# Feed-forward down product: all eleven pairs of k tiles by seven products, in three rounds

## The chip, the cores and the metric

The kernel runs on one core of one Trainium2 chip. The metric is the device time of one execution in microseconds (us). The core has a matrix engine (PE, with its weight loads shown as PEld), a vector engine (DVE), a scalar engine (ACT), a general engine (POOL) and a queue engine that only starts transfers (SP). Each of them executes its own list of instructions in a fixed order; semaphores hold an instruction back until what it needs is there.

## The reference, cut to what matters

The program is a trunk of two layers on 512 tokens of width 1024: a state-space mixer (SSD), a feed-forward block (FFN), latent attention (MLA), and a second FFN. After every block the residual stream `h` is normalised.

```python
def conv_ffn(h, up, conv_w, conv_b, down):          # hidden width 2816
    u = causal_depthwise_conv(h @ up, conv_w, conv_b)
    g, val = jnp.split(u, 2, axis=-1)
    return (jax.nn.silu(g) * val) @ down

for i in range(DEPTH):                               # DEPTH = 2
    mix = ssd_mixer(...) if i < N_A_LAYERS else mla_attention(...)
    h = layer_norm(DN_ALPHA * h + mix, ln_mix_g[i], ln_mix_b[i])
    ff = conv_ffn(h, ffn_up[i], ffn_conv_w[i], ffn_conv_b[i], ffn_down[i])
    h = layer_norm(DN_ALPHA * h + ff, ln_ffn_g[i], ln_ffn_b[i])
```

The change is in the product with `down`, 512 tokens x 2816 x 1024, in both FFN blocks, and in the normalisation that follows it.

## The kernel before, in words

**Precision.** Every product is made of three matmuls: each operand is kept as a rounded high part and a low remainder (hi, lo), and hi x hi, hi x lo and lo x hi are added in PSUM. `mm_b` (L162) issues these three for one stationary tile of 128 tokens and 512 output columns. Its first matmul needs the high part of the weight, its second the low part.

**The weight stream.** `WStream` (L31) walks one long list of items, the weights in the order in which products use them. SP loads an item into one of six staging buffers. `_split` (L76) makes the high part on ACT (L96, a cast) and the low part on DVE (L97, a subtraction) in one of six pairs of buffers (`nb`), and then `fill` (L59) starts further loads. `ahead(i)` (L102) splits items up to `la` (4) places beyond `i`, but never more than six beyond the last retired item. `retire` (L112) wants the items in order.

**The hidden width.** 2816 is 22 k tiles of 128. For each k tile the kernel makes two products with `up`, the convolution and the gate (`conv3_silu_gate`, L321, called by `finish`).

**Seven products for a pair.** An even and an odd k tile, two halves of the tokens (256 each) and two halves of the output columns (512 each) form a 2 x 2 by 2 x 2 block product. It is done with seven products instead of eight. `pair_operands` (L344) makes the operands a11, a12, a22, s1, s2, s3, s4 on the token side. On the weight side the operands are sums, kept in the tiles `rs` (`sums`), one for each part of a round (a part is one or two pairs that share an item). The kinds of an item say how it arises: "r" is loaded into `rs`; "a" is added to `rs` by an accumulating DMA which POOL issues (L52); "+" is added on DVE (L88); "=" uses the loaded tile itself; "-" is `rs` minus the loaded tile on DVE (L91); no kind is a plain load. An accumulating DMA can start only when every reader of `rs` before it is done.

**The rounds.** `RP0` and `RP1` (L288) give two rounds: five pairs in parts of 2, 2 and 1, then four pairs in parts of 2, 1 and 1. `down_pairs` (L361) runs a round: a11, s1, s2 and s4 in turn, s3, a12, a22, each over all parts, and adds each result to `h` on DVE (L387). Its inner `ahead` wraps the splits in `issue_after(ins)`, so that their DVE instructions come behind the add just issued. The last four k tiles have no pairs: after round two they are multiplied plainly, one token tile after another and the two column halves in turn (L525 to L555), with the items of 1024 columns held for all four token tiles. Each of these adds (`add_mix`, L175, L185) also sums the row for the mean.

**Normalisation.** For token tile i: `ln_mean` (L189, DVE), a square with a row sum on ACT (L194), `ln_a` (two halves on DVE, L210), the variance (L203, on DVE in the second FFN, on POOL in the first) and a power on POOL (L204), then `ln_b` (two halves, L215), which stands behind the first add of the next token tile. In the first FFN `transpose_h` (L266) turns a finished tile by eight PE transposes (L274) into `ht`, with a cast on ACT (L277) and a subtraction on DVE (L278); the last two transposes are done inside MLA. MLA's first product, `down(0)` (L1155), reads tile 0 of `ht`, the third matmul already its low part. In the second FFN the last token tile goes through `ln_last` (L231), which takes its second column half as two matmul groups of 256 columns, adds them at L243 and L251, and ends the kernel.

**Order.** SP's list is in the order of the program text. The lists of the other engines are made by a planner at compile time: whenever an engine is free in its plan, the ready instruction that stands first in the program text goes next. `issue_after` forbids the instructions in its block, on that one engine, to stand ahead of the given instruction.

Of the kernel before, what the change touches and what calls it, by code (L numbers as in the profile page):

```python
# [18 lines left out]
P = 128  # L19
# [11 lines left out]
class WStream:  # L31
# [5 lines left out]
    def __init__(self, k, items, nb, nst, la):  # L37
        self.k, self.items, self.nb, self.nst, self.la = k, items, nb, nst, la
        self.out = 0
        self.split = 0  # L40
        self.done = 0
        self.st = {}
        self.w = {}

# [67 lines left out]
    def retire(self, i):  # L112
        assert i == self.done
        del self.w[i]
        self.done += 1
# [172 lines left out]
RP0 = ((2, 2, 1), (2, 1, 1))  # L288
RP1 = ((2, 2, 1), (2, 1, 1))


def rounds(rp):
    r0 = 2 * sum(rp[0])
    return r0, r0 + 2 * sum(rp[1])


def ffn_items(up, down, rp):
# [3 lines left out]
    it = []  # L301
    R0, R1 = rounds(rp)
    dv = down.rearrange("(k p) n -> p k n", p=P)
    for r, ks in enumerate((range(R0), range(R0, HT))):
        for c in ks:
            it.append((up[c], 1024))
            it.append((up[c + HT], 1024))

        for odd, hf, kinds in ((0, 0, "r"), (0, 1, "a"), (1, 1, "+="), (0, 0, "-"), (1, 0, None), (1, 0, "a")):
            j = ks[0]  # L310
            for p, n in enumerate(rp[r]):
# [49 lines left out]
def down_pairs(k, ws, n, prs, parts, first, between):  # L361

    nc = k.nc
    X, Y, Z = ([k.bank() for _ in range(2)] for _ in range(3))
    ni = len(parts)
    at = [sum(parts[:p]) for p in range(ni + 1)]
    new = {(i, hf) for i in range(NT) for hf in range(2)} if first else set()  # L370

    def product(bs, op, p, i, start, stop):
        wh, wl = ws.get(i, 3)
        ps = prs[at[p]:at[p + 1]]
        for t in range(2):
            for q, pr in enumerate(ps):
                x, c0 = pr[op]
                sl = slice(q * 512, (q + 1) * 512)
                k.mm_b(bs[t], x, slice(c0 + t * P, c0 + (t + 1) * P), wh[:, sl], wl[:, sl],
                       start and p == 0 and q == 0, stop and p == ni - 1 and q == len(ps) - 1)  # L380
        ws.retire(i)

    def add(bs, row, hf, sign):
        for t in range(2):
            i = 2 * row + t
            hs = k.h[:, i, hf * 512:(hf + 1) * 512]
            last = nc.vector.scalar_tensor_tensor(hs, hs, ALPHA if (i, hf) in new else 1.0, bs[t], op0=ALU.mult,  # L387
                                                  op1=ALU.add if sign > 0 else ALU.subtract)
            new.discard((i, hf))
        return last  # L390

    def ahead(n, ins):

        with k.tc.issue_after(ins.ins):
            ws.ahead(n)

    for p in range(ni):
        product(X, "a11", p, n + p, True, True)
    n += ni
    ahead(n, add(X, 0, 0, 1))  # L400
    for p in range(ni):
        product(Y, "s1", p, n + p, True, True)
    n += ni
    ahead(n, add(Y, 1, 1, 1))
    between()
    for p in range(ni):
        product(X, "s2", p, n + 2 * p, False, True)
        product(Y, "s4", p, n + 2 * p + 1, False, True)
    n += 2 * ni
    add(X, 0, 1, -1)  # L410
    ahead(n, add(Y, 0, 1, 1))
    for bs, op, s0, out in ((X, "s3", False, (1, 1, -1)), (Z, "a12", True, (0, 0, 1)), (X, "a22", False, (1, 0, 1))):
        for p in range(ni):
            product(bs, op, p, n + p, s0, True)
        n += ni
        ahead(n, add(bs, *out))
    return n


def ffn(k, ws, base, cwp, gb, rp, la=2, out=None, mid=None):  # L420

    nc, tc = k.nc, k.tc
    R0, R1 = rounds(rp)
    with ExitStack() as c:
        pool = lambda n, b: c.enter_context(tc.tile_pool(name=n, bufs=b))
        pools = {"gt": pool("gt", 18), "fw": pool("fw", 7), "rs": pool("rs", 1), "cw": pool("cw", 1)}
# [8 lines left out]
        ws.sums = [rs[:, 0], rs[:, 1], pools["rs"].tile([P, 512], F32, name="rs2")]  # L435
# [9 lines left out]
        for r in range(2):  # L445
            gts, prs = [], []
# [4 lines left out]
            def finish(ci, bg, bv):  # L451
                if ci >= R1:
                    gts.append(new_gt())
                    conv3_silu_gate(k, pools, bg, bv, cw, ci, gts[-1])
                    return
# [10 lines left out]
            c0 = r * R0  # L466
# [21 lines left out]
            for ci in range(c0, HT if r else R0):  # L488
# [11 lines left out]
            n = down_pairs(k, ws, n, prs, rp[r], not r, norm_params if r else lambda: None)  # L500
        if out is None:
            k.new_ht()

        nk = HT - R1
        nw = nk // 2

        def piece(i, b, hf, c0, c1, retire):
            for jc in range(nw):
                wh, wl = ws.get(n + hf * nw + jc)
                for jj in range(2):  # L510
                    j = jc * 2 + jj
                    o = slice(jj * 512 + c0, jj * 512 + c1)
                    k.mm_b(b, gts[j], slice(i * P, (i + 1) * P), wh[:, o], wl[:, o], j == 0, j == nk - 1)
                if retire:
                    ws.retire(n + hf * nw + jc)

        xn = {}
# [961 lines left out]
```

## Time and profile before

| | |
|---|---|
| median of 3 runs | 1307.37 us (1306.93 to 1308.01) |
| time of the profiled execution | 1306.91 us |
| its span, first to last instruction | 1305.2 us |
| mean granted clock of TensorE | 0.998 |
| instructions: PE, DVE, ACT, POOL | 6570, 1605, 1022, 88 |
| bytes moved by DMA | 147.72 MB, 113 GB/s on average |

The profile is one execution. A row of its timeline has the start in us, the busy time in us, the engine, the line of the kernel, the operation, what it writes and reads, and the count of merged instructions; in brackets stands the idle time before it and what ended that. A row of its view by windows has the stretch, its length, the busy time (and count) of PE, PEld, DVE, ACT and POOL, the granted clock of TensorE, the mean busy share of the DMA engines and GB/s.

### The profile page before, as it was taken

To read this page: it belongs to the slowest core of one execution; us is meant where nothing else is said; L and a number is where in the kernel's file an instruction comes from. 1 tells how busy PE (TensorE), PEld (TensorE's weight loads), DVE (VectorE), ACT (ScalarE), POOL (GpSimd) and SP (SyncE) were. 2 spreads that over 40 slices of the span, in tenths; PEclk is the share of its full clock that TensorE was granted. 3 is DMA by queue.
4 is the path that set the end of the run, shared out by engine and by line. 5 is a ranking of instruction groups with operands and counts; after the bars stand their busy time and mean duration, and the time that the engine had idled before them with its cause. 6 is when DMAs were issued, how large, how long until landed. Compare 5 with 4: busy or idle time off the path is not lost.

```text
span 1305.2 us, 17262 instructions
## 1 busy us (share of the span) xinstructions
PE 1296.5 (99%) x6570; PEld 1100.7 (84%) x6570; DVE 1008.0 (77%) x1605; ACT 630.7 (48%) x1022; POOL 67.5 (5%) x88
## 2 busy tenths in 40 slices
PE   9999999999999999999999999999999999999997
PEld 8888888888888988888888899888898888888886
DVE  7788888787799868866766876898587786667587
ACT  6766545536533544444443434665254444444341
POOL 0000000000001001100000012000100000000000
PEclk9999999999999999999999999999999999999999
DMA  8533323324411433352312721231054226333251
GB/s 298 192 125 114 142 101 102 131 73 144 161 62 68 130 129 81 76 206 95 126 63 33 249 89 61 70 109 49 17 180 137 69 40 208 129 97 105 41 162 64
DMA packets 52082, 147.72 MB, mean 113 GB/s; under 512 B 5568, under 2 KB 8640, under 8 KB 50720
## 3 DMA queue, kind: packets, MB, share of 16 engines
q1 hardware_dynamic: 46784, 136.71, 30.5%
q0 software_dynamic: 5072, 9.77, 4.4%
q8 instruction: 51, 0.84, 0.3%
q14 instruction: 31, 0.25, 0.1%
q10 hardware_dynamic: 144, 0.15, 0.0%
HBM read 144.44 MB, written 2.16 MB: 112 GB/s over the span
## 4 chain that ended last, share of the span: by engine, by line
PE 99%; DVE 0%; issue 0%; ACT 0%; DVEq 0%; ACTq 0%
PE ps L159 58%; PE ps L165 10%; PE ps L167 10%; PE ps L166 10%; PE ps L1276 2%; PE ps L800 1%; PE ps L1317 1%; PE ps L925 1%; PE ps L274 1%; PE ps L816 1%; PE ps L1299 1%; PE ps L789 1%; PE ps L743 1%; PE ps L767 1%; PE ps L620 0%; PE ps L838 0%
## 5 line engine op out<-in xcount | busy, mean ns | idle before, releaser
L159 PE MATMUL ps<-ht,wh 128*128 128x512 f32 (+1 forms) x2256 | 517.1, 379 | 0.0
L159 PEld LDWEIGHTS ps<-ht,wh 128*128 128x128 f32 x2256 | 408.1, 188 | 79.6 <-issue 1.4
L97 DVE TENSOR_TENSOR wl<-wst,wh 128x1024 fp32r<-128x1024 f32 (+3 forms) x222 | 253.4, 1158 | 39.8 <-ACT wh L96 38.7
L96 ACT CAST wh<-wst 128x1024 fp32r<-128x1024 f32 (+3 forms) x222 | 218.7, 995 | 125.3 <-PE ps L167 68.5
L159 PE MATMUL ps<-ht,wl 128*128 128x512 f32 (+1 forms) x1128 | 266.7, 379 | 0.0
L159 PEld LDWEIGHTS ps<-ht,wl 128*128 128x128 f32 x1128 | 205.2, 188 | 39.7
L328 DVE SCALAR_TENSOR_TENSOR acc<-ps,cw,acc 128x511 f32<-128x511 f32 x88 | 65.7, 747 | 80.1 <-ACT acc L327 80.1
L165 PE MATMUL ps<-wh,gt 128*128 128x512 f32 (+1 forms) x320 | 123.7, 387 | 0.0
L167 PE MATMUL ps<-wh,gt 128*128 128x512 f32 (+1 forms) x320 | 123.6, 386 | 0.0
L166 PE MATMUL ps<-wl,gt 128*128 128x512 f32 (+1 forms) x320 | 123.6, 386 | 0.0
L340 ACT CAST gt<-acc 128x512 fp32r<-128x512 f32 (+1 forms) x80 | 44.0, 571 | 101.9 <-DVE acc L333 99.3
L327 ACT ACTIVATE acc<-ps,cw 128x512 f32<-128x512 f32 x88 | 68.3, 776 | 29.5 <-PE ps L159 29.4
L658 DVE SCALAR_TENSOR_TENSOR cv<-ps,cw,cv 128x511 f32<-128x511 f32 (+2 forms) x72 | 53.7, 745 | 21.7 <-ACT cv L656 21.1
L166 PEld LDWEIGHTS ps<-wl,gt 128*128 128x128 f32 x320 | 60.1, 188 | 12.2
L165 PEld LDWEIGHTS ps<-wh,gt 128*128 128x128 f32 x320 | 60.1, 188 | 12.2
L167 PEld LDWEIGHTS ps<-wh,gt 128*128 128x128 f32 x320 | 60.1, 188 | 12.1
L332 ACT ACTIVATE acc<-acc 128x512 f32<-128x512 f32 x44 | 27.8, 632 | 87.6 <-DVE acc L329 87.4
L329 DVE SCALAR_TENSOR_TENSOR acc<-ps,cw,acc 128x510 f32<-128x510 f32 x88 | 65.8, 747 | 2.5
L96 ACT CAST wh<-rs 128x1024 fp32r<-128x1024 f32 (+1 forms) x48 | 39.9, 834 | 46.1 <-DVE rs L88 27.1
L341 DVE TENSOR_TENSOR gt<-acc,gt 128x512 fp32r<-128x512 f32 (+1 forms) x80 | 48.7, 627 | 13.5 <-ACT gt L340 13.5
L387 DVE SCALAR_TENSOR_TENSOR h<-h,ps 128x512 f32<-128x512 f32 x56 | 37.5, 685 | 25.6 <-PE ps L167 25.6
L52 POOL DMA_DIRECT2D rs<-in_down_dram x24 | 25.1, 1045 | 576.1 <-DVE wl L97 576.1
(248 smaller groups left out, 1727.2 us busy)
## 6 DMA issues: line engine op xcount, KB each, us to landing
wst<-in_up_dram SPq DMA_DIRECT2D x88, 512.0 KB, 3.5
wst<-in_xbc_dram SPq DMA_DIRECT2D x32, 512.0 KB, 6.3
wst<-in_down_dram SPq DMA_DIRECT2D x26, 512.0 KB, 5.8
W<-cumd SPq DMA_DIRECT2D x8, 1024.0 KB, 4.7
wst<-in_sow_dram SPq DMA_DIRECT2D x16, 512.0 KB, 3.5
wst<-in_zw_dram SPq DMA_DIRECT2D x14, 512.0 KB, 6.0
rs<-in_down_dram POOLq DMA_DIRECT2D x12, 512.0 KB, 6.9
wst<-in_down_dram SPq DMA_DIRECT2D x18, 256.0 KB, 2.6
```

Source lines behind the costliest of these rows:

```text
L96: nc.scalar.copy(h[:, :f], s[:, :f])
L97: nc.vector.tensor_tensor(l[:, :f], s[:, :f], h[:, :f], op=ALU.subtract)
L159: nc.tensor.matmul(out, w[:, k, :], xts[k][:, x, ts], start=first and p == 0 and k == 0, stop=last and p == 2 and k == nk - 1, skip_group_ ...
L165: nc.tensor.matmul(out, xt[:, 0, tsl], wh, start=start, stop=False, skip_group_check=True)
L166: nc.tensor.matmul(out, xt[:, 0, tsl], wl, start=False, stop=False, skip_group_check=True)
L167: nc.tensor.matmul(out, xt[:, 1, tsl], wh, start=False, stop=stop, skip_group_check=True)
L327: nc.scalar.activation(a, b, AF.Identity, bias=cw[:, ch, 3:4], scale=cw[:, ch, 2:3])
L328: nc.vector.scalar_tensor_tensor(a[:, 1:], b[:, :SEQ - 1], cw[:, ch, 1:2], a[:, 1:], op0=ALU.mult, op1=ALU.add)
L329: nc.vector.scalar_tensor_tensor(a[:, 2:], b[:, :SEQ - 2], cw[:, ch, 0:1], a[:, 2:], op0=ALU.mult, op1=ALU.add)
L340: k.nc.scalar.copy(dst[:, 0, :], src)
L341: k.nc.vector.tensor_tensor(dst[:, 1, :], src, dst[:, 0, :], op=ALU.subtract)
L658: nc.vector.scalar_tensor_tensor(t[:, d:], b[:, :SEQ - d], cw[:, ch, 3 - d:4 - d], t[:, d:], op0=ALU.mult, op1=ALU.add)
```

## The change

All 22 k tiles become eleven pairs, in three rounds of four, three and four pairs, in parts (2, 2), (2, 1) and (2, 2). The plain product of the last four k tiles is gone, and with it the third tile of sums. `down_pairs` becomes a class `Pairs`. In every round a11 and s1 are now interleaved part by part, so the items are no longer retired in order, and `retire` allows that. In the last round the column halves are exchanged and the items of a12 stand ahead of those of s3. That round ends one token tile at a time: a12 for tiles 0 and 1, then s3 and a22 for tile 2, s3 and a22 for tile 3, where a22 starts in banks of its own. The normalisation is placed between these. `ln_last` is kept.

```diff
     def retire(self, i):
-        assert i == self.done
         del self.w[i]
-        self.done += 1
+        self.gone.add(i)
+        while self.done in self.gone:
+            self.gone.remove(self.done)
+            self.done += 1
...
-RP0 = ((2, 2, 1), (2, 1, 1))
-RP1 = ((2, 2, 1), (2, 1, 1))
+RP = ((2, 2), (2, 1), (2, 2))
...
+HEAD = ((0, 0, "r"), (0, 1, "a"), (1, 1, "+="))
+TAIL = ((0, 0, "-"), (1, 0, None), (1, 0, "a"))
...
+        last = r == len(rp) - 1
+        for odd, hf, kinds in HEAD + ((TAIL[1], TAIL[0], TAIL[2]) if last else TAIL):
+            j = at[r]
+            hf = 1 - hf if last else hf
...
-    for hf in range(2):
-        for j in range(R1, HT, 2):
-            it.append((dv[:, j:j + 2, hf * 512:(hf + 1) * 512], 1024))
...
+    def ahead(self, ins):
+
+        with self.k.tc.issue_after(ins.ins):
+            self.ws.ahead(self.n)
+
+    def half(self, between, f, last=False):
+
+        X, Y, ni = self.X, self.Y, self.ni
         for p in range(ni):
-            product(bs, op, p, n + p, s0, True)
-        n += ni
-        ahead(n, add(bs, *out))
-    return n
+            self.product(X, "a11", p, self.n + p, True)
+            if p == ni - 1:
+                a = self.adds(X, 0, f, 1)
+                with self.k.tc.issue_after(a.ins):
+                    self.ws.ahead(self.n + 2 * ni - 1)
+            self.product(Y, "s1", p, self.n + ni + p, True)
+        self.n += 2 * ni
+        self.ahead(self.adds(Y, 1, 1 - f, 1))
+        between()
+        for p in range(ni):
+            self.product(X, "s2", p, self.n + 2 * p, False)
+            self.product(Y, "s4", p, self.n + 2 * p + 1, False)
+        self.n += 2 * ni
+        self.adds(X, 0, 1 - f, -1)
+        self.ahead(self.adds(Y, 0, 1 - f, 1, last))
...
+            if r < len(rp) - 1:
+                pp = Pairs(k, ws, n, prs, rp[r], not r)
+                pp.half(lambda: None, 0)
+                n = pp.rest()
...
+        pp = Pairs(k, ws, n, prs, rp[-1], False)
+        ni = pp.ni
+        pp.half(norm_params, 1, True)
+        for t in range(2):
+            for p in range(ni):
+                pp.tile(pp.Z[t], "a12", p, pp.n + p, t, True)
+                if t:
+                    ws.retire(pp.n + p)
+            a = pp.add(pp.Z[t], t, 1, 1, True)
+            if t:
+                with tc.issue_after(a.ins):
+                    ln_b(0, 0)
+                    ln_b(0, 1)
+            ln_a(t)
+        pp.n += ni
+        pp.ahead(a)
+        for t in range(2):
+            i = 2 + t
+            for p in range(ni):
+                pp.tile(pp.X[t], "s3", p, pp.n + p, t, False)
+                if t:
+                    ws.retire(pp.n + p)
+            pp.add(pp.X[t], i, 0, -1, True)
+            a = pp.add(pp.X[t], i, 1, 1)
+            with tc.issue_after(a.ins):
+                ln_b(i - 1, 0)
+                if out is None or not t:
+                    ln_b(i - 1, 1)
+            if t:
+                with tc.issue_after(a.ins):
+                    ws.ahead(pp.n + 2 * ni, la)
+                if out is None:
+                    k.transpose_h(0)
+            cuts = ((0, 256), (256, 512)) if t and out is not None else ((0, 512),)
+            bs = [k.bank()[:, :c1 - c0] for c0, c1 in cuts]
+            for b, (c0, c1) in zip(bs, cuts):
+                for p in range(ni):
+                    pp.tile(b, "a22", p, pp.n + ni + p, t, True, c0, c1)
+                    if t and c1 == 512:
+                        ws.retire(pp.n + ni + p)
+            if len(bs) > 1:
+                k.ln_last(i, bs, out[i * P:(i + 1) * P, :], lambda: ln_b(i - 1, 1))
+                continue
+            if t:
+                ws.ahead(pp.n + 2 * ni, la)
+            pp.add(bs[0], i, 1, 1, True)
+            if t:
+                k.transpose_h(1)
+            ln_a(i)
```

The method `tile` issues the matmuls of one part for one token tile, `add` adds one bank to `h` (with the row sum if `last`), `adds` does so for both tiles of a product, and `rest` runs s3, a12 and a22 of the first two rounds as before.

More of the change, by code (lines that the diff above doesn't have):

```diff
@@ L358, in pair_operands @@
     split(k, s34, v)
[L361 to L374, printed above, removed]
-        for t in range(2):
[L376 to L383, printed above, removed]
-        for t in range(2):
[L385 to L398, printed above, removed]
-    n += ni
[L400 to L412, printed above, removed]
-        for p in range(ni):
-            product(bs, op, p, n + p, s0, True)
-        n += ni
-        ahead(n, add(bs, *out))
-    return n
@@ new lines, with __init__, tile, product @@
+class Pairs:
+    def __init__(self, k, ws, n, prs, parts, first):
+        self.k, self.ws, self.n, self.prs, self.parts, self.first = k, ws, n, prs, parts, first
+        self.ni = len(parts)
+        self.at = [sum(parts[:p]) for p in range(self.ni + 1)]
+        self.new = {(i, hf) for i in range(NT) for hf in range(2)} if first else set()
+        self.X, self.Y, self.Z = ([k.bank() for _ in range(2)] for _ in range(3))
+    def tile(self, out, op, p, i, t, start, c0=0, c1=512):
+        wh, wl = self.ws.get(i, 3)
+        ps = self.prs[self.at[p]:self.at[p + 1]]
+        for q, pr in enumerate(ps):
+            x, o = pr[op]
+            sl = slice(q * 512 + c0, q * 512 + c1)
+            self.k.mm_b(out, x, slice(o + t * P, o + (t + 1) * P), wh[:, sl], wl[:, sl],
+                        start and p == 0 and q == 0, p == self.ni - 1 and q == len(ps) - 1)
+    def product(self, bs, op, p, i, start):
+        for t in range(2):
+            self.tile(bs[t], op, p, i, t, start)
+        self.ws.retire(i)
+    def add(self, b, i, hf, sign, last=False):
+        k = self.k
+        kw = {}
+        if last:
+            if i not in k.st:
+                k.st[i] = k.small.tile([P, 6], F32, name="lnst", bufs=4)
+            kw["accum_out"] = k.st[i][:, hf:hf + 1]
+        hs = k.h[:, i, hf * 512:(hf + 1) * 512]
+        a = k.nc.vector.scalar_tensor_tensor(hs, hs, ALPHA if (i, hf) in self.new else 1.0, b, op0=ALU.mult,
+                                             op1=ALU.add if sign > 0 else ALU.subtract, **kw)
+        self.new.discard((i, hf))
+        return a
+    def adds(self, bs, row, hf, sign, last=False):
+        for t in range(2):
+            a = self.add(bs[t], 2 * row + t, hf, sign, last)
+        return a
+    def ahead(self, ins):
[3 more added lines that the diff above has]
+        X, Y, ni = self.X, self.Y, self.ni
+        for p in range(ni):
+            self.product(X, "a11", p, self.n + p, True)
[13 more added lines that the diff above has]
+        self.ahead(self.adds(Y, 0, 1 - f, 1, last))
+    def rest(self):
+        for bs, op, s0, out in ((self.X, "s3", False, (1, 1, -1)), (self.Z, "a12", True, (0, 0, 1)), (self.X, "a22", False, (1, 0, 1))):
+            for p in range(self.ni):
+                self.product(bs, op, p, self.n + p, s0)
+            self.n += self.ni
+            self.ahead(self.adds(bs, *out))
+        return self.n
@@ L487, in ffn @@
                 c0 += 2
-            for ci in range(c0, HT if r else R0):
+            for ci in range(c0, at[r + 1]):
                 bg, bv = k.bank(), k.bank()
```

90 lines of the change are left out of this document (27 added, 63 removed).

## The prediction

> **What bounds the kernel now.** I read the page first: the busy shares and the chain of waits.
>
> ```profile
> PE 1296.5 (99%) x6570; PEld 1100.7 (84%) x6570; DVE 1008.0 (77%) x1605; ACT 630.7 (48%) x1022; POOL 67.5 (5%) x88
> ...
> PE 99%; DVE 0%; issue 0%; ACT 0%; DVEq 0%; ACTq 0%
> ```
>
> PE never pauses, so every matmul removed can shorten the run. But DVE is at 77% on average, and the windows view shows where it stands higher: the up stage before round two, round two, and the plain tail with its normalisation, in the first FFN.
>
> ```profile
> 577.40:707.90 130.50, 130.50 (x577) 108.12 (x576) 88.19 (x122) 56.72 (x78) 2.92 (x3) 1.00 0.32 98
> 707.90:746.00 38.10, 38.10 (x169) 31.56 (x169) 30.83 (x40) 17.96 (x23) 2.96 (x3) 1.00 0.59 182
> 746.00:769.50 23.50, 23.50 (x114) 19.61 (x112) 20.46 (x38) 9.16 (x13) 2.65 (x6) 1.00 0.29 94
> ```
>
> After the stretch and its length, the first busy time is PE's and the third is DVE's: 88 of 130, 31 of 38, and 20.5 of 23.5 in the tail. The change takes PE time out of that last stretch, so the question is whether DVE can follow.
>
> The timeline of PE gives the price of a matmul and the fixed points of the second FFN: round two starts at 1237.43, the last token tile's half-width matmuls at 1294.55, the last one at 1297.30.
>
> ```profile
> 1237.43 0.39 PE L165 MATMUL ps<-wh,gt 128*128 128x512 f32 x1
> ...
> 1294.55 0.28 PE L165 MATMUL ps<-wh,gt 128*128 128x256 f32 x1
> ...
> 1297.30 0.28 PE L167 MATMUL ps<-wh,gt 128*128 128x256 f32 x1
> ```
>
> Four pairs are 7 x 4 x 2 x 3 = 168 matmuls, the tail up to 1294.55 has 84: 57.12 / 252 = 0.2267 us each. The 23 steps to the last one give 0.12 for half width.
>
> **The change: what PE saves.** Four plain k tiles cost 4 x 4 x 2 x 3 = 96 matmuls, two pairs 84. Two FFNs save 24 x 0.2267 = 5.44 us. Nothing else is taken from PE.
>
> **What DVE gains, and where.** Call E the end of s4 in the last round. Before, PE had 72 matmuls of pairs and 96 of the tail left after s4, 38.1 us. Now it has 72 in all: 16.3 us. Into these go the normalisation of tiles 0 to 2 and, by the order of the text, weight splits. The DVE timeline of the second FFN shows the rule by which splits are placed.
>
> ```profile
> 1234.19 0.68 DVE L88 TENSOR_TENSOR rs<-rs,wst 128x512 f32<-128x512 f32 x1
> ...
> 1242.47 1.28 DVE L387 SCALAR_TENSOR_TENSOR h<-h,ps 128x512 f32<-128x512 f32 x2
> 1243.67 1.22 DVE L88 TENSOR_TENSOR rs<-rs,wst 128x1024 f32<-128x1024 f32 x1
> 1244.93 1.23 DVE L91 TENSOR_TENSOR wst<-rs,wst 128x1024 f32<-128x1024 f32 x1
> 1246.08 1.23 DVE L97 TENSOR_TENSOR wl<-rs,wh 128x1024 fp32r<-128x1024 f32 x1
> 1247.22 1.22 DVE L97 TENSOR_TENSOR wl<-wst,wh 128x1024 fp32r<-128x1024 f32 x1
> ...
> 1257.35 2.73 DVE L387 SCALAR_TENSOR_TENSOR h<-h,ps 128x512 f32<-128x512 f32 x4 [0.65 <-PE ps L167]
> 1259.99 1.82 DVE L97 TENSOR_TENSOR wl<-wst,wh 128x1024 fp32r<-128x1024 f32 x2
> ```
>
> The sum of part 1 (512 wide, 1234.19) ran nine us ahead of that of part 0 (1243.67), because only the latter is split inside the `issue_after` of the a11 adds (1242.47). Likewise the splits at 1259.99 stand right behind the four adds of s2 and s4. E was 1237.43 + 96 x 0.2267 = 1259.19, so the last of these adds ended at E + 0.89 (1260.08).
>
> I number the items of the new last round 0 to 13: a11 0, 1; s1 2, 3; s2 and s4 4 to 7; a12 8, 9; s3 10, 11; a22 12, 13. While s4 runs, `get` with look-ahead 3 reaches item 10. Items 11 and 12 come from `ahead` behind the s4 adds, 13 from `ahead` behind the second a12 add. So after E + 0.89 DVE has one L91 (item 11) and three L97: 1.15 + 3 x 1.14 = 4.57 us, by the steps 1244.93 to 1246.08 to 1247.22. Then come adds and normalisation:
>
> ```profile
> 1269.59 1.37 DVE L387 SCALAR_TENSOR_TENSOR h<-h,ps 128x512 f32<-128x512 f32 x2 [1.73 <-PE ps L167]
> 1270.87 1.22 DVE L97 TENSOR_TENSOR wl<-wst,wh 128x1024 fp32r<-128x1024 f32 x1
> ...
> 1281.15 0.69 DVE L185 SCALAR_TENSOR_TENSOR h<-h,ps 128x512 f32<-128x512 f32 x1 [2.02 <-PE ps L167]
> ...
> 1281.88 0.21 DVE L189 TENSOR_SCALAR lnst<-lnst 128x1 f32<-128x1 f32 x1
> 1282.13 1.42 DVE L210 SCALAR_TENSOR_TENSOR xn<-h,lnst,lng 128x512 f32<-128x512 f32 x2
> 1283.46 0.15 DVE L203 TENSOR_SCALAR lnst<-lnst 128x1 f32<-128x1 f32 x1
> ...
> 1296.18 0.42 DVE L243 SCALAR_TENSOR_TENSOR h<-h,ps 128x256 f32<-128x256 f32 x1
> ...
> 1297.87 0.41 DVE L251 SCALAR_TENSOR_TENSOR h<-h,ps 128x256 f32<-128x256 f32 x1
> ```
>
> An add with mean, `ln_a` and variance is 1281.15 to 1283.61, 2.46 us. Two adds are 1.28, and 0.08 more with a row sum (the subtracting add with a row sum has no row; its price lies between 0.64 and the 0.73 of L185, I take 0.72). An `ln_b` pair is 1.32 (767.94 to 769.26, below).
>
> **Second FFN, in DVE's order from E:** 0.89; weights 4.57; tile 0 2.46; tile 1 with `ln_b` of tile 0 3.78; two s3 adds and `ln_b` 2.68; tile 2 2.46; two s3 adds and half an `ln_b` 2.02; from L243 to L251 1.69 as before. That is 20.55. Every piece is there by its turn (PE delivers tile 1 at 5.44, s3 of tile 2 at 8.2), so DVE does not pause. PE alone would allow L251 at 60 x 0.2267 + 24 x 0.12 + 0.45 (1297.42 to 1297.87) = E + 16.93. DVE is late by 3.62, and the end moves with L251.
>
> **First FFN.** `down(0)` follows the last transposes on PE, and its third matmul needs the low part of tile 0 of `ht`.
>
> ```profile
> 768.69 1.03 PE L274 MATMUL ps<-ident,h 128*128 128x128 f32 x8
> 769.48 0.42 PE L165 MATMUL ps<-wh,ht 128*128 128x384 f32 x1
> ...
> 769.91 0.34 PE L167 MATMUL ps<-wh,ht 128*128 128x384 f32 x1
> ```
>
> ```profile
> 764.21 1.28 DVE L278 TENSOR_TENSOR ht<-ps,ht 128x512 fp32r<-128x512 f32 x2
> 765.40 0.74 DVE L210 SCALAR_TENSOR_TENSOR xn<-h,lnst,lng 128x512 f32<-128x512 f32 x1
> ...
> 767.94 1.41 DVE L215 SCALAR_TENSOR_TENSOR h<-xn,lnst,lnb 128x512 f32<-128x512 f32 x2
> 769.26 2.95 DVE L97 TENSOR_TENSOR wl<-wst,wh 128x1024 fp32r<-128x1024 f32 x3
> 772.14 0.68 DVE L185 SCALAR_TENSOR_TENSOR h<-h,ps 128x512 f32<-128x512 f32 x1
> 772.74 1.28 DVE L278 TENSOR_TENSOR ht<-ps,ht 128x512 fp32r<-128x512 f32 x2
> ```
>
> Before, the low part of tile 0 was there at 765.4, 4.5 us ahead of its use, and the add and transposes of the last tiles could stand behind three splits (769.26) at no cost. Now tile 0's transposes stand behind `ws.ahead(..., la)`, in the text after s3 of tile 3. In DVE's order: 0.89; weights 4.57; four more L97 for MLA's first items (14 to 17) 4.56; tile 0 2.31 (no L203 on DVE here); tile 1 and `ln_b` 3.63; s3 adds and `ln_b` 2.68; tile 2 2.31; s3 adds and `ln_b` 2.68; the first L278 0.60: E + 24.2. PE alone would reach `down(0)` at 16.32 + 2 x 0.79 = E + 17.9 and its third matmul 0.43 later (769.48 to 769.91). DVE is late by 5.90.
>
> Sum, on the profiled execution: 1306.91 - 5.44 + 3.62 + 5.90 = 1310.99. The median lies 0.46 above that execution: **1311.5 us**.
>
> **The accumulating DMA of a22.** Item 13 reaches `rs` by a DMA that waits for L91 of item 11, at E + 2.04.
>
> ```profile
> 1244.98 1.06 ACT L96 CAST wh<-rs 128x1024 fp32r<-128x1024 f32 x1 [3.15 <-DVE rs L88]
> ...
> 1247.69 1.20 POOL L52 DMA_DIRECT2D rs<-in_down_dram  x1 [23.88 <-DVE wl L97]
> ...
> DMA to landing us min/median/max: 3.9/6.5/9.3
> ```
>
> POOL starts 0.38 after the DVE end (1247.31), landing takes 6.5 (3.9 to 9.3), the cast 1.06, L97 1.2: E + 11.6 (9.0 to 14.4). PE wants the low part after 43 matmuls, E + 9.75, so it waits up to 4.7, likely 1.9, in each FFN. DVE's list has L97 of item 13 done at 11.7 anyway, so this wait lies inside the lateness above; it costs 3.8 in all only if DVE keeps pace. Behind item 13's cast on ACT stand the squares, and behind its L97 on DVE the s3 adds: with a landing of 9.3 DVE stands for up to 14.4 - 11.7 = 2.7 more, and with 3.9 for nothing.
>
> **What I cost at nothing.** The other rounds: a round of (2, 2) keeps 38.1 us of PE and gets some 33 of DVE (the 30.8 above, with the last pair's operands in and less narrow splits out); one of (2, 1) has 28.6 of PE and about 29 of DVE, and the surplus falls into an up stage with 42 us free (577.40). Without that cover the cost is 1 us a round. s1 of part 0 is now wanted 2.7 us after the start, but its items are split a whole up tile (10.9) earlier. s2 reuses the banks of a11, whose adds must be done; 1 us remains in the (2, 1) round. On SP the normalisation's two loads stand behind MLA's item loads, which wait for L97 to free staging; that eats the margin in the first FFN only, and late they would add to DVE's lateness.
>
> **Rivals.** (a) The clock. In the first FFN, with the 1.9 of the a22 wait, PE is through its transposes at about E + 19.8 and stands some 4 us until E + 24.2. What an idle PE does is seen after the last matmul:
>
> ```profile
> 1299.40:1300.40 1.00, 0.00 (x0) 0.00 (x0) 1.00 (x2) 0.00 (x0) 0.84 (x1) 0.90 0.12 45
> 1300.40:1301.40 1.00, 0.00 (x0) 0.00 (x0) 1.00 (x3) 0.00 (x0) 0.00 (x0) 0.50 0.00 0
> ```
>
> The clock falls to half about 2.8 us after PE's end (1297.42). If it falls here too and needs as long to come back, the first 2.8 us of `down(0)` do half their work: 1.4 more, 1312.9. No stall inside this run shows the fall or the return.
>
> [...]
>
> (b) Not slower: DVE keeps pace, since the planner lets the transposed tile and `ln_last` go ahead of splits, and only the a22 wait is left: -5.44 + 3.8, 1305.7. It needs 3.6 and 5.9 us less on DVE than my lists. For it: each list is a sum of pitches, 10% too long would be 2 us of each. Against it: the rows above stand in text order.
>
> (c) Full gain: the splits of item 11 are done before E as well, nothing waits: 1301.9. Against it stands 1259.99.
>
> **How the numbers follow.** Forecast 0.43, between 1309.5 and 1314; (a) 0.14; (b), with its neighbours from 1305 to 1309.5, 0.26; (c) 0.13; both lists late by another 1 to 2, 0.04. A difference of 0.2%, 2.6 us, is about what can be told from none. Of (b), 0.19 lies within it, and of the forecast 0.04. (c) and 0.07 of (b) give faster 0.20; same 0.23; slower 0.57. The range from 1303.5 to 1315 leaves out (c) and the far end.
>
> **What would show it.** 12 matmuls fewer per FFN. After s4 of the last rounds, DVE without a pause up to L251 and L278; PE waiting in a22 of tile 2 for L97 of item 13 (some 2 us) and before `down(0)` (some 4). Wrong: idle DVE in those stretches, L91 of item 11 ahead of the s4 adds, or PE waits in the first two rounds.

## The result, and the profile after

The changed kernel takes 1323.13 us (median of 4 runs, 1322.45 to 1324.41), the kernel before 1307.53 us beside it. The ratio is 1.0123 (95% interval 1.011 to 1.0135): slower by 15.6 us. The prediction said slower, by 4.1 us, and its range ended at 1315.

The profiled execution took 1322.45 us, its span is 1320.4 us against 1305.2. First the page of the changed kernel: busy times with instruction counts, and the shares of the chain that ended last.

```profile
PE 1297.5 (98%) x6546; PEld 1098.8 (83%) x6546; DVE 1033.3 (78%) x1637; ACT 635.9 (48%) x1022; POOL 71.6 (5%) x88
...
PE 96%; DVE 2%; issue 1%; ACT 0%; DMA 0%; POOL 0%; SPq 0%; DVEq 0%; ACTq 0%
```

PE has 24 matmuls fewer, as planned, but it is no longer the whole chain. What it waited for stands in the view of PE's waits (what waited, for what, us in total, times, longest):

```profile
PE ps L169 <- DVE wl L98: 5.2, 2, 3.1
PE ps L170 <- DVE ht L281: 2.9, 1, 2.9
PE ps L277 <- DVE h L218: 2.8, 1, 2.8
```

In the kernel before this view had no such rows. The line numbers are those of the changed kernel: L168 to L170 are the three matmuls of `mm_b`, L97 the cast and L98 the subtraction of a weight split, L92 the "-" of an item, L53 the accumulating DMA, L400 an add to `h`, L192 the mean, L197 the square, L206 and L207 variance and power, L213 `ln_a`, L218 `ln_b`, L277 the transposes, L280 and L281 their high and low part, L246 and L254 the two adds of `ln_last`.

The first row is the low part of item 13, the last weights of a22, once in each FFN. The other two stand at the start of MLA. Up to the last round of the first FFN only about 1 us had been lost; it began at 728.10 us, that of the second at 1267.60. E, the end of s4, is 96 matmuls later, at 749.86 and 1289.36. The windows view answers the prediction's main question, how long DVE's list is behind E. The first stretch reaches from E to the low part of tile 0 of `ht`, the second from E to L254; the third busy time is DVE's.

```profile
749.86:778.50 28.64, 19.88 (x97) 16.02 (x95) 23.23 (x39) 14.55 (x20) 3.87 (x7) 0.98 0.37 101
1289.36:1311.90 22.54, 18.57 (x85) 15.18 (x83) 18.05 (x39) 6.68 (x9) 3.88 (x4) 0.92 0.28 70
```

DVE has 23.2 and 18.1 us of work there, in stretches of 28.6 and 22.5. So it stood idle for 5.4 and 4.5 us, on the path. Of these 9.9 us, 7.7 are waits for a variance or power (3.35 + 0.98 in the first FFN, 2.62 + 0.46 + 0.33 in the second), and the rest are waits for PE's results. The timeline of DVE in the first FFN shows where (start, busy time, engine, line; in brackets the idle time before it and what ended that):

```profile
750.67 1.22 DVE L92 TENSOR_TENSOR wst<-rs,wst 128x1024 f32<-128x1024 f32 x1
752.78 0.69 DVE L400 SCALAR_TENSOR_TENSOR h<-h,ps 128x512 f32<-128x512 f32 x1 [0.89 <-PE ps L170]
...
757.72 0.21 DVE L192 TENSOR_SCALAR lnst<-lnst 128x1 f32<-128x1 f32 x1
761.28 1.41 DVE L218 SCALAR_TENSOR_TENSOR h<-xn,lnst,lnb 128x512 f32<-128x512 f32 x2 [3.35 <-POOL lnst L207]
...
763.93 1.22 DVE L98 TENSOR_TENSOR wl<-rs,wh 128x1024 fp32r<-128x1024 f32 x1
...
774.19 1.41 DVE L218 SCALAR_TENSOR_TENSOR h<-xn,lnst,lnb 128x512 f32<-128x512 f32 x2 [0.98 <-POOL lnst L207]
775.52 2.35 DVE L98 TENSOR_TENSOR wl<-wst,wh 128x1024 fp32r<-128x1024 f32 x2
777.79 1.28 DVE L281 TENSOR_TENSOR ht<-ps,ht 128x512 fp32r<-128x512 f32 x2
```

The pause of 3.35 us is a wait for the variance of tile 0, which needs the square from ACT. ACT's and POOL's timelines of the same stretch:

```profile
752.49 1.20 POOL L53 DMA_DIRECT2D rs<-in_down_dram  x1 [25.77 <-DVE wst L92]
```

```profile
752.06 1.05 ACT L97 CAST wh<-wst 128x1024 fp32r<-128x1024 f32 x1 [8.69 <-DVE wst L92]
...
758.12 1.05 ACT L97 CAST wh<-rs 128x1024 fp32r<-128x1024 f32 x1 [4.05 <-DMA rs<-in_down_dram]
759.08 1.14 ACT L197 ACTIVATE lnjunk<-h,lnst 128x1024 bf16<-128x1024 f32 x1
```

ACT's list has the cast of item 13 ahead of the square of tile 0. The cast stood 4.05 us until the accumulating DMA had landed (752.49 to 758.12, 5.6 us), and the square behind it with it. Item 13's own subtraction on DVE came only at 763.93, behind the delayed `ln_b` and another `ln_a`. The second FFN repeats it: its cast started at 1297.70, 5.7 us after POOL's issue at 1291.99, and DVE stood 2.62 us for the square:

```profile
1297.70 1.05 ACT L97 CAST wh<-rs 128x1024 fp32r<-128x1024 f32 x1 [4.13 <-PE ps L170]
```

```profile
1299.92 0.15 DVE L206 TENSOR_SCALAR lnst<-lnst 128x1 f32<-128x1 f32 x1 [2.62 <-ACT lnjunk L197]
```

(The view there names a PE instruction as the cast's releaser; PE had been done with that buffer for 8 us, so I take it for the DMA again.)

The clock fell, too. Windows of two microseconds at the start of MLA, and behind the a22 wait of the second FFN; the third number from the end is the granted clock:

```profile
776.00:778.00 2.00, 0.00 (x0) 0.00 (x0) 2.00 (x3) 0.27 (x1) 0.00 (x0) 0.82 0.17 11
778.00:780.00 2.00, 1.47 (x5) 1.47 (x6) 2.00 (x4) 0.00 (x0) 0.00 (x0) 0.50 0.75 247
...
784.00:786.00 2.00, 2.00 (x15) 2.00 (x14) 1.29 (x2) 0.07 (x1) 1.09 (x2) 0.98 0.17 67
...
1302.00:1304.00 2.00, 2.00 (x8) 1.64 (x7) 2.00 (x4) 0.00 (x0) 0.00 (x0) 0.73 0.29 110
1304.00:1306.00 2.00, 2.00 (x6) 1.54 (x6) 2.00 (x6) 0.00 (x0) 0.55 (x1) 0.50 0.40 153
1306.00:1308.00 2.00, 2.00 (x14) 1.78 (x13) 2.00 (x5) 0.00 (x0) 0.00 (x0) 0.92 0.33 125
```

### The profile page after: what moved, and what is told of

It reads as the page before. It is cut to its first block, busy times and chain, and to the rows that moved or that the text cites. A ratio compares the mean times of both kernels' runs of the same rounds, so it can differ in the third digit from the quotient of the medians.

```text
span 1320.4 us, 17213 instructions
## 1 busy us (share of the span) xinstructions
PE 1297.5 (98%) x6546; PEld 1098.8 (83%) x6546; DVE 1033.3 (78%) x1637; ACT 635.9 (48%) x1022; POOL 71.6 (5%) x88
## 4 chain that ended last, share of the span: by engine, by line
PE 96%; DVE 2%; issue 1%; ACT 0%; DMA 0%; POOL 0%; SPq 0%; DVEq 0%; ACTq 0%
PE ps L162 58%; PE ps L170 9%; PE ps L169 9%; PE ps L168 9%; PE ps L1312 2%; PE ps L836 1%; PE ps L1353 1%; PE ps L852 1%; PE ps L277 1%; DVE wl L98 1%; PE ps L1335 1%; PE ps L825 1%; PE ps L961 1%; PE ps L779 1%; PE ps L803 1%
## 5 line engine op out<-in xcount | busy, mean ns | idle before, releaser
L98 DVE TENSOR_TENSOR wl<-wst,wh 128x1024 fp32r<-128x1024 f32 (+2 forms) x214 | 250.0, 1186 | 36.4 <-ACT wh L97 36.2
L97 ACT CAST wh<-wst 128x1024 fp32r<-128x1024 f32 (+2 forms) x214 | 213.1, 1016 | 131.1 <-PE ps L170 52.8
L170 PE MATMUL ps<-wh,gt 128*128 128x512 f32 (+1 forms) x312 | 121.2, 389 | 0.0
L168 PE MATMUL ps<-wh,gt 128*128 128x512 f32 (+1 forms) x312 | 120.2, 389 | 0.0
L348 ACT CAST gt<-acc 128x256 fp32r<-128x256 f32 (+1 forms) x88 | 47.8, 566 | 107.4 <-DVE acc L341 98.1
L97 ACT CAST wh<-rs 128x1024 fp32r<-128x1024 f32 (+1 forms) x48 | 46.7, 978 | 59.0 <-DMA rs<-in_down_dram 23.0
L98 DVE TENSOR_TENSOR wl<-rs,wh 128x1024 fp32r<-128x1024 f32 (+1 forms) x48 | 54.4, 1133 | 23.4 <-ACT wh L97 23.2
L168 PEld LDWEIGHTS ps<-wh,gt 128*128 128x128 f32 x312 | 59.0, 189 | 12.7 <-ACT gt L348 0.4
L170 PEld LDWEIGHTS ps<-wh,gt 128*128 128x128 f32 x312 | 58.8, 189 | 12.3 <-DVE gt L349 0.5
L400 DVE SCALAR_TENSOR_TENSOR h<-h,ps 128x512 f32<-128x512 f32 x87 | 57.2, 682 | 13.0 <-PE ps L170 12.8
L53 POOL DMA_DIRECT2D rs<-in_down_dram x24 | 27.7, 1194 | 630.7 <-DVE wl L98 512.1
```

The lines of the kernel that those rows point to most:

```text
L97: nc.scalar.copy(h[:, :f], s[:, :f])
L98: nc.vector.tensor_tensor(l[:, :f], s[:, :f], h[:, :f], op=ALU.subtract)
L168: nc.tensor.matmul(out, xt[:, 0, tsl], wh, start=start, stop=False, skip_group_check=True)
L170: nc.tensor.matmul(out, xt[:, 1, tsl], wh, start=False, stop=stop, skip_group_check=True)
L348: k.nc.scalar.copy(dst[:, 0, :], src)
L400: a = k.nc.vector.scalar_tensor_tensor(hs, hs, ALPHA if (i, hf) in self.new else 1.0, b, op0=ALU.mult, op1=ALU.add if sign > 0 else ALU.su ...
```

## The experiments

Each short diff is against the changed kernel or the run named. The kernel before ran beside them each time (medians 1307.05 to 1307.95, against 1307.53 beside the changed kernel), so differences in us between runs of different sets are uncertain by some tenths; the ratios to the kernel before are not. "Tile 0 first" below is what the expectations call the run with the transposes first.

**Splits ahead of the adds.** This takes away the lateness of the accumulating DMA and part of DVE's list at once.

```diff
         self.n += 2 * ni
+        self.ws.ahead(self.n if last else 0)
         self.adds(X, 0, 1 - f, -1)
         self.ahead(self.adds(Y, 0, 1 - f, 1, last))
```

> Beside the changed kernel (1323.1 us), the two last pieces before the accumulating load (the subtraction for the second half of s3's weights, and the split of that piece and of the first half of a22's) are called ahead of the adds of s2 and s4 instead of behind them. Theory A (the VectorE list behind s4 is simply too long, it never had to stand idle): 1.2 + 2 x 1.06 = 3.3 us less of list in each feed-forward, so about 1323.1 - 6.6 = 1316.5, and the idle time of VectorE in the two tails stays as it is. Theory B (the last accumulating load lands late, its cast on ScalarE stands ahead of the squares of the layer norm, and VectorE stands idle for them): the load is issued some 5 us earlier, the idle time of VectorE in both tails (3.35 + 0.98 and about 3.4 us) goes as well, and with it the half-speed clock that follows the stalls: 1305 to 1311.

Measured: 1311.1 us (1310.64 to 1311.56), 12.0 us less than the changed kernel; 1.0029 of before (1.0017 to 1.004). The "-" moved from 750.67 to 738.30 us, far ahead of s4. The waits of PE that are left in this run:

```profile
PE ps L170 <- DVE ht L281: 2.9, 1, 2.9
...
PE ps L277 <- DVE h L218: 0.9, 1, 0.9
```

The wait for item 13 is gone, and DVE waits for POOL's power 3.7 us in the whole run instead of 8.1. The time is at the edge of what theory B gave and well below theory A. The half clock, which theory B let go as well, did not go: it lasted some 3.4 us from 773.8 us on (0.50 from 774 to 776 us). And both parts of the edit work here, so the next runs take them apart.

**No accumulating DMA for a22.**

```diff
-        for odd, hf, kinds in HEAD + ((TAIL[1], TAIL[0], TAIL[2]) if last else TAIL):
+        for odd, hf, kinds in HEAD + ((TAIL[1], TAIL[0], (1, 0, None)) if last else TAIL):
```

> Leaves out a part of the computation: the second weights of a22 in the last round are loaded plainly instead of being accumulated onto the sum (a22 multiplies the lower right weights alone). Every instruction on TensorE, VectorE and ScalarE stays, in number and size; only the waits for the two accumulating loads per feed-forward go. Theory A (list too long): within 2 us of the changed kernel, 1321 to 1323. Theory B (the late load idles VectorE and so TensorE): the weight waits of TensorE (5.2 us in two) and most of VectorE's idle time in the tails go, 4.3 us in the first feed-forward and some 3 in the second, and up to 4 us of half-speed clock behind them: 1312 to 1317. If it falls lower than about 1312 the accumulating loads alone were the whole loss.

Measured: 1315.33 us (1315.08 to 1315.56), 7.8 us less, with the same work on PE, DVE and ACT; POOL issues four DMAs fewer. DVE's pauses for variance and power in the two tails fell from 4.3 and 3.4 us to 1.4 and 0.8. Theory A has no place for this.

**The squares ahead of the waiting cast.** The DMA stays; only the order on ACT and DVE differs.

```diff
         pp.n += ni
-        pp.ahead(a)
+        with tc.issue_after(k.ln_sq.ins): pp.ahead(a)
```

> The split of the last piece of a22 (cast on ScalarE, low part on VectorE), which waits for the accumulating load, stands behind the squares of token tiles 0 and 1 on ScalarE instead of ahead of them; its low part falls behind the adds of s3 for tile 2 on VectorE. The load itself lands when it did. Theory B in its narrow form (the cast that waits for the load blocks ScalarE's queue, and VectorE starves for the squares): VectorE's idle time of 3.35 us in the first feed-forward and some 2.6 in the second falls to under 1 us, and the end comes 3 to 6 us earlier: 1317 to 1320. Theory B in its wide form (TensorE waits for the load itself): the wait for the last a22 piece stays at 2 to 3 us in each and the time within 1.5 us of 1323. Theory A: 1323.

Measured: 1316.4 us (1315.49 to 1316.99), 6.7 us less. ACT's timeline in the first FFN of this run:

```profile
756.14 1.15 ACT L197 ACTIVATE lnjunk<-h,lnst 128x1024 bf16<-128x1024 f32 x1 [1.91 <-DVE lnst L192]
...
760.34 1.15 ACT L197 ACTIVATE lnjunk<-h,lnst 128x1024 bf16<-128x1024 f32 x1 [2.95 <-DVE lnst L192]
...
761.48 1.03 ACT L97 CAST wh<-rs 128x1024 fp32r<-128x1024 f32 x1
```

The square of tile 0 starts at 756.14 instead of 759.08, the cast 3.4 us later than before, and PE waits 0.6 us for item 13 in both tails together. So most of the 7.8 us that the DMA costs comes through ACT's queue: an instruction that waits for a DMA stood at its head (4.05 us in the changed kernel), and work that was ready stood behind it. The narrow form holds, the wide one doesn't.

**MLA's splits behind the transposes.**

```diff
             if t:
+                if out is None:
+                    a = k.transpose_h(0)
                 with tc.issue_after(a.ins):
                     ws.ahead(pp.n + 2 * ni, la)
-                if out is None:
-                    k.transpose_h(0)
```

> In the first feed-forward the splits of the two first 128x1024 pieces of the attention stage's weights stand behind the transposes of the first token tile instead of ahead of them. 2 x 1.06 = 2.1 us of VectorE's work move behind the low part of tile 0 of the transposed activations, on which the attention stage's first products wait. Theory A and B alike: the stall at that place falls from 5.65 to some 3.5 us, -2.1 us. Theory C (the half-speed clock that follows, some 2.6 us, hangs on how long TensorE stood): with a stall of 3.5 us the clock holds or falls for a shorter time, another 1 to 2.6 us: 1318.5 to 1320; without it 1321. The second feed-forward stays as it is.

Measured: 1320.82 us median, but four runs from 1317.79 to 1322.52. PE's wait for L281 fell from 2.9 to 0.6 us, as worked out. The profiled execution is the fastest of the four, with a mean clock of 0.996 against 0.993 and 0.992 in two others. Its windows at the place where the changed kernel ran at half clock:

```profile
776.00:778.00 2.00, 2.00 (x13) 2.00 (x14) 2.00 (x3) 0.01 (x1) 0.00 (x0) 1.00 0.00 0
778.00:780.00 2.00, 2.00 (x14) 2.00 (x14) 2.00 (x3) 0.00 (x0) 0.00 (x0) 1.00 0.51 135
```

With pauses of 2.6 and 0.6 us the clock held here. That the other executions lost theirs at this place is argued from their mean clock; there is no trace of them.

**The clock by itself.**

```diff
             if t:
-                k.transpose_h(1)
+                a = k.transpose_h(1)
+                if out is None:
+                    b = k.bank()
+                    with tc.issue_after(a.ins):
+                        for _ in range(22):
+                            nc.tensor.matmul(b[:, :P], k.ident, k.ident, start=True, stop=True)
```

> The changed kernel as it is (1323.1 us, with all its waits), and 22 matmuls of the unit matrix by itself, whose result nobody reads, in TensorE's list of the first feed-forward behind the transposes of tile 1, where TensorE stands 2.8 and 2.9 us in the changed kernel. They are about 22 x 0.23 = 5.0 us long and fill the stall without shortening it. Theory C (a part of the loss is the half-speed clock that follows that stall, some 6 us at 0.50): the granted clock between 775 and 786 us stays near 1.0 and the time falls by 2 to 3 us, to 1320 to 1321. If the clock falls all the same (for the pause at 762 us, or for another reason): 1323.

Measured: 1321.31 us (1320.92 to 1322.59), 1.8 us less. The filling matmuls (each recorded as two) and the windows of this run:

```profile
772.91 5.08 PE L595 MATMUL ps<-ident 128*128 128x128 f32 x44
```

```profile
760.00:768.00 8.00, 4.81 (x16) 3.55 (x15) 6.74 (x10) 4.26 (x7) 1.94 (x4) 0.82 0.10 16
768.00:772.00 4.00, 4.00 (x22) 3.29 (x21) 4.00 (x10) 2.86 (x4) 0.00 (x0) 0.94 0.49 162
...
778.00:780.00 2.00, 1.07 (x8) 0.82 (x7) 2.00 (x4) 0.58 (x1) 0.00 (x0) 1.00 0.24 36
```

The half clock at the start of MLA is gone, and the time is lower: theory C, though the ranges of the two kernels (four runs each) overlap a little. In this execution the clock fell earlier instead, for some 3.4 us around 766 us, behind the a22 wait of 3.2 us, where the changed kernel's profile shows 1.00. That made the transposes and what hangs on them late, and MLA's third matmul started at 780.01 instead of 778.53 us. So the 1.8 us understate what the fall at MLA costs. From that third matmul to the first round of the second FFN it is 269.51 us in the changed kernel, 266.99 here and 267.32 with MLA's splits behind the transposes, where the clock held as well: 2.2 to 2.5 us.

**Tile 0 first.** On top of the early splits, the transposes of tile 0 are called ahead of `ln_b` of tile 2 and ahead of MLA's splits.

```diff
+            if t and out is None:
+                a = k.transpose_h(0)
             with tc.issue_after(a.ins):
                 ln_b(i - 1, 0)
...
-                if out is None:
-                    k.transpose_h(0)
```

> The early split as before (1311.1 us), and in the first feed-forward the two transposes of token tile 0 and their copies called ahead of the closing layer-norm step of tile 2 and ahead of the splits of the attention stage's weights. Theory D (what is left of the loss in the first feed-forward is the place of the low part of tile 0 in VectorE's list, behind 1.33 us of layer norm and 2.28 us of splits): TensorE's waits of 2.9 us (for the low part) and 0.9 us (for the layer norm ahead of the transposes of tile 2) go, 3.8 us: 1307.3. Rival: the work that is pushed behind (layer norm of tile 2, splits of the attention weights) is wanted 2 to 4 us later and makes a wait of its own: 1309 to 1311. The end, in the second feed-forward, stays 9.85 us behind the last matmul.

Measured: 1306.65 us (1306.13 to 1307.63), 0.9996 of before (0.9986 to 1.0005). Both waits are gone; DVE's timeline at that place:

```profile
767.80 1.28 DVE L281 TENSOR_TENSOR ht<-ps,ht 128x512 fp32r<-128x512 f32 x2
769.00 1.40 DVE L218 SCALAR_TENSOR_TENSOR h<-xn,lnst,lnb 128x512 f32<-128x512 f32 x2
770.33 4.09 DVE L98 TENSOR_TENSOR wl<-wst,wh 128x1024 fp32r<-128x1024 f32 x4
```

Theory D holds: two edits of order, no instruction less, take 16.5 us and leave a kernel that can't be told from the one before.

**The small round first.**

```diff
-RP = ((2, 2), (2, 1), (2, 2))
+RP = ((2, 1), (2, 2), (2, 2))
```

> As the run with the transposes first, and the round of three pairs is the first of the three instead of the second. In the order of the change TensorE paused 0.53 us in each of the two small rounds, where s2 and s4 wait for banks and weights behind a11 and s1 of three pairs only. Theory E (the pause belongs to the small round wherever it stands): no difference within 0.3 us. Theory F (it belongs to what VectorE has to do at that place): up to 1.1 us less, or more if the first round has more to do beside it (in it the two first chunks are split at 256 columns and the rope tables are made).

Measured: 1306.89 us (1306.15 to 1308.09), no difference. A round of three pairs needs 126 x 0.2267 = 28.56 us; it took 29.1 in the second place (1140.44 to 1169.55 us with tile 0 first) and 29.1 in the first place (487.54 to 516.66). The half microsecond belongs to the small round, wherever it stands: theory E.

**Whole products.** One part of the change undone: a12 and s3 finish both token tiles together.

```diff
-            for p in range(ni):
-                pp.tile(pp.Z[t], "a12", p, pp.n + p, t, True)
-                if t:
-                    ws.retire(pp.n + p)
+            if not t: [pp.product(pp.Z, "a12", p, pp.n + p, True) for p in range(ni)]
```

(and the same for s3)

> As the run with the transposes first, but the part 'one token tile at a time' undone for a12 and s3: both token tiles of a product are finished together, as in the other rounds. The sum of tile 0 comes 6 x 0.2267 x 2 = 2.7 us later in a12, tile 2 of s3 as well. If VectorE's list sets the end, it stands idle that much longer behind s4 and the end moves by 2 to 2.7 us in each feed-forward: 1311 to 1313 beside 1307.3. If TensorE alone set the end there: no difference.

Measured: 1310.45 us (1308.9 to 1311.4), 3.8 us more than with tile 0 first, a little less than expected. PE waits again at MLA's start:

```profile
PE ps L170 <- DVE ht L281: 2.5, 1, 2.5
```

"One token tile at a time" is worth its place: it was not what made the change slow.

**`ln_b` of tiles 0 and 1 off DVE.**

```diff
-            k.ln_b(i, f, xn[i])
+            if i < 2:
+                x, fs = xn[i], slice(f * 512, (f + 1) * 512)
+                nc.scalar.activation(x[:, fs], x[:, fs], AF.Identity, scale=k.st[i][:, 5:6])
+                k.ln_end = nc.gpsimd.tensor_tensor(k.h[:, i, fs], x[:, fs], k.gb[1][:, fs], op=ALU.add)
+            else:
+                k.ln_b(i, f, xn[i])
```

> As the run with the transposes first, and for token tiles 0 and 1 the closing layer-norm step leaves VectorE: ScalarE scales by the reciprocal deviation (two 128x512 per tile), GpSimd adds the bias (two 128x512 per tile). 4 x 0.66 = 2.6 us of VectorE's list go in each feed-forward. Theory A' (what is left in the second feed-forward is the length of VectorE's list ahead of the last adds: last matmul to end is 9.85 us there against 7.3 in the kernel before): 2 to 2.5 us less at the end, and the rest of the first feed-forward's stall: 1303 to 1305, which would be faster than the kernel before. Rival (GpSimd's adds, whose time no trace here shows, or their use of SBUF beside VectorE, hold up what waits for them): no gain, or slower than the run with the transposes first.

Measured: 1307.29 us (1306.7 to 1307.78), 0.6 us more than with tile 0 first; the rival holds. (That no trace has such an add on POOL was wrong: the rope's add of 128x512 stands in both traces with 1.42 us on average.) The groups view over the second tail (1280 to 1306 us), first with tile 0 first, then in this run (busy us, mean ns):

```profile
L400 DVE SCALAR_TENSOR_TENSOR h<-h,ps 128x512 f32<-128x512 f32 x7 | 4.7, 681 | 2.0 <-PE ps L170 1.9
...
L213 DVE SCALAR_TENSOR_TENSOR xn<-h,lnst,lng 128x512 f32<-128x512 f32 x6 | 4.2, 748 | 0.0
```

```profile
L213 DVE SCALAR_TENSOR_TENSOR xn<-h,lnst,lng 128x512 f32<-128x512 f32 x6 | 7.4, 1268 | 0.1
L400 DVE SCALAR_TENSOR_TENSOR h<-h,ps 128x512 f32<-128x512 f32 x7 | 4.6, 680 | 2.0 <-PE ps L170 1.9
```

```profile
L541 POOL TENSOR_TENSOR h<-xn,lnb 128x512 f32<-128x512 f32 x4 | 6.4, 1628 | 1.7 <-ACT xn L540 1.7
```

Four `ln_b` halves left DVE, 2.6 us by their steps, and 3.2 came back in `ln_a`, which grew from 748 to 1268 ns a half, while the adds out of PSUM stayed at 680. Most of these adds ran when POOL did not add; the first FFN has one that ran wholly beside POOL's adds (763.95 us). DVE and POOL there, and for `ln_a` in the second FFN:

```profile
763.95 0.67 DVE L400 SCALAR_TENSOR_TENSOR h<-h,ps 128x512 f32<-128x512 f32 x1
...
1286.40 3.24 DVE L213 SCALAR_TENSOR_TENSOR xn<-h,lnst,lng 128x512 f32<-128x512 f32 x2
```

```profile
762.93 3.95 POOL L541 TENSOR_TENSOR h<-xn,lnb 128x512 f32<-128x512 f32 x2 [0.83 <-ACT xn L540]
...
1285.64 3.45 POOL L541 TENSOR_TENSOR h<-xn,lnb 128x512 f32<-128x512 f32 x2 [0.84 <-ACT xn L540]
```

**One add for s3 and a22.** s3 runs for tiles 2 and 3 first, then a22 accumulates in the same banks; `ln_b` of tile 2 moves behind a22.

```diff
-            pp.add(pp.X[t], i, 0, -1, True)
-            a = pp.add(pp.X[t], i, 1, 1)
+            a = pp.add(pp.X[t], 2 + t, 0, -1, True)
...
-            bs = [k.bank()[:, :c1 - c0] for c0, c1 in cuts]
+            bs = [pp.X[t][:, c0:c1] for c0, c1 in cuts]
...
-                    pp.tile(b, "a22", p, pp.n + ni + p, t, True, c0, c1)
+                    pp.tile(b, "a22", p, pp.n + ni + p, t, False, c0, c1)
```

> As the run with the transposes first (1306.65 us), but in the closing pair of products s3 is made for both tiles 2 and 3 first and a22 then accumulates onto the same banks, as the earlier rounds do; so the sum of s3 and a22 is added to the lower right quarter in one step instead of two, and two adds of 128x512 (0.61 us from one to the next) leave VectorE's list in each feed-forward. Tile 2 is complete one half-product (12 x 0.2267 = 2.7 us) later. Theory A' (from s4 to the end VectorE's list is the bound, so work taken off it comes off the end): 1.2 us less at the end, about 1305.4, ahead of the kernel before by 0.1 to 0.2%. Rival (the later tile 2 pushes its layer norm into the tail, 1.3 us): no gain, 1306.5. And if VectorE were no bound any more after the two edits: no difference.

Measured: 1306.12 us (1305.73 to 1306.68), 0.9987 of before (0.9978 to 0.9996). The time lies between theory and rival. The gain did not come at the end: from the last matmul's end (1294.92) to the end of the span it is 10.0 us, against 9.7 with tile 0 first. There the rival was right.

**The same in the first FFN alone**, the second as with tile 0 first.

> The run with one add (1306.1 us) in the first feed-forward, the run with the transposes first (1306.65 us) in the second. In the one-add run the attention stage's output product started 0.4 us earlier than in the run with the transposes first although the last round began 0.5 us later, while from the last matmul to the end it took 10.1 us instead of 9.7, and the second feed-forward took 0.3 us longer up to that matmul. Theory: the later completion of tile 2 costs in the second feed-forward, where the layer norm of tile 2 falls into the tail, and gains in the first, where it does not: 1306.1 - 0.7 = 1305.4 us. Rival: these differences are no more than what one profile differs from the next, 1306.1 to 1306.6.

Measured: 1305.77 us (1305.15 to 1306.68), 0.9984 of before (0.9975 to 0.9993): 2.2 us faster than the kernel before on the same chip. The interval leaves out 1, though the gain is below the 0.2% that the prediction took for a difference. Between the last three versions (tile 0 first, one add, this one) the differences are of the size of their intervals; which of them is best isn't settled.

## Why the prediction was wrong

It failed above all in one step: "Every piece is there by its turn (PE delivers tile 1 at 5.44, s3 of tile 2 at 8.2), so DVE does not pause." DVE paused for 9.9 us. What was not there was, above all, the variance of tile 0, whose chain over ACT and POOL the lists left out. Its square stood behind a cast that waited for a DMA. In the run without that DMA 2.2 of the 7.7 us of waits for variance and power are left, in waits of 0.33 to 0.72 us; the lists left these out too. PE's pieces were there but for a short wait: the cast of item 11 on ACT (752.06 us) comes between its "-" and its subtraction, the planner put the first a12 add into that place, and this add stood 0.89 us for PE (the row at 752.78, and the same in the second FFN). In numbers, against the sum on record (span against span, +15.2 measured):

| step | predicted | measured |
|---|---|---|
| matmuls saved | -5.44 | -5.44 (24 fewer, rounds of four pairs took 38.1 us) |
| DVE's list later than PE, first FFN | +5.90 | 23.2 - 18.3 = +4.9 |
| the same, second FFN | +3.62 | 18.1 - 16.9 = +1.1 |
| DVE's pauses | 0 | 5.4 + 4.5 = +9.9 |
| half clock | 0 (rival: +1.4) | +1.8 (run with the filling matmuls; 2.2 to 2.5 by the profiles) |
| order behind L254 | 0 | 8.5 - 7.33 = +1.2 |
| rounds of three pairs | 0 | +0.53 and +0.55 |
| up to the first round of the first FFN | 0 | +0.5 |

The column adds up to 15.0 with the 1.8, 0.2 less than the span shows, and to 15.4 to 15.7 with the figures from the profiles. Without the pauses and the half clock it would stand at +3.3, close to the +4.1 forecast; that is in part luck, since lists that were 3.5 too long made up for 2.8 us in the last three rows that had been put at nothing. The +0.5 ahead of the first round (508.58 us) is no more than executions differ there: 507.9 with the early splits.

- *Where the splits stand.* Right for the "-" of item 11, which came directly behind the s4 adds (750.67 us, E + 0.81). The subtractions of items 11 and 12 came behind the first a12 add, that of item 13 only at 763.93.
- *The lengths of the lists.* Right in kind, too long in size: E + 24.2 and E + 20.55 against 23.2 and 18.1 us of work. I had added steps that contained short waits between adds and small instructions. In the second FFN I had also put both halves of tile 2's `ln_b` ahead of L251; one of them (0.66 us) ran behind L254, at 1312.55, and is a part of the +1.2 there.
- *The accumulating DMA.* The prediction had every part of it: "Behind item 13's cast on ACT stand the squares". It priced them at nothing, since "this wait lies inside the lateness above". That held PE's wait against DVE's list, but not the square against DVE's next instruction. The landing was even shorter than assumed, 5.6 against 6.5 us. (Its terms add up to E + 11.2, from 8.6 to 14.0, and not to E + 11.6; PE's wait for item 13 is then 1.4 instead of 1.9 us and rival (b) 0.8 lower. The forecast does not use it.) Making the squares go first took 6.7 us off, taking the DMA away 7.8.
- *PE's waits.* "Some 2" in a22 of tile 2: 2.1 and 3.1. "Some 4" before `down(0)`: 2.8 + 2.9.
- *The clock.* Rival (a) happened, on top of the forecast and not in place of it. "Needs as long to come back" was too short: the half clock lasted 6.8 us at MLA (0.72 + 6 + 0.08 by the windows) and 3.4 in the second FFN (1.08 + 2 + 0.32).
- *Rivals (b) and (c).* Neither happened by itself. (c), "the splits of item 11 are done before E as well", is what the early split makes, and it gave 1311.1 and not 1301.9: the list was still the bound.
- *The range.* All that was put at nothing made the kernel slower when it came, so a range that reached further down than up missed it.

Open: of 5.44 us that PE saves, the best version keeps 2.2. With tile 0 first, MLA starts 1.9 us earlier than in the kernel before and its output product only 0.45 us (897.03 against 897.48), and the end comes 9.7 us behind the last matmul instead of 7.6. The traces show a part of the first: MLA's third matmul is only 1.37 us earlier (768.54 against 769.91), and PE then waits 0.4 and 0.2 us at the transposes of L1232, where the kernel before has no wait. No run tested these, and no edit shortened the second.

## What to carry to other kernels

When a stage gets shorter on its bounding engine, list what the second engine waits for, not only what it has to do: every chain over a third engine (square, variance, power) belongs into the list with its latency. An instruction that waits for a late DMA holds up what stands behind it in its engine's fixed order (here a cast on ACT stood 4.05 us, and the square of tile 0 behind it; with the squares ahead of it the run took 6.7 us less), so look for it at the head of each queue and move either the issue earlier or the ready work ahead. Moving a transfer's trigger and a tile's last copy forward was worth more here (16.5 us) than the matmuls the change saved (5.44).

## What the runs showed of the hardware

- *The clock fell to half behind a pause of 2.1 us, and held behind longer ones.* In the second FFN of the changed kernel PE waited 2.1 us by its row (one matmul at 1298.88, the next at 1301.38 us), and the granted clock fell to 0.50 1.5 us after work had gone on; with whole products a pause of 2.48 us had no fall behind it (1.00 from 768 to 786 us). The a22 wait of the first FFN had none behind it in the changed kernel (3.14 us; 1.00 from 760 to 776 us) and one with the filling matmuls (3.19 us; 0.82 from 760 to 768 us). So the length of the pause alone did not decide it. The seven falls with work behind them that the windows show lasted about 3.4 or 6.8 us: 6.8 and 3.4 in the changed kernel, 6.8 with the squares first and without the accumulating DMA, 3.4 with the early splits and, twice, in the run with the filling matmuls. Why there are these two lengths, and why pauses of nearly the same length (3.14 and 3.19 us) had a fall in one run and none in the other, no run here shows.
- *`ln_a` on DVE took longer beside POOL's adds; the one add out of PSUM that ran beside them did not.* Two `ln_a` halves, which read `h` and `lng`, took 3.24 us instead of 1.42 beside two adds on POOL. The one add to `h` out of PSUM that ran wholly beside POOL's adds took 0.67 us, no longer than the others (0.68). Whether the place of the operands makes this difference no run tested.
